# Seven block products for two of three down-projections, and the sample tile moved to the first block

## The chip, the cores and the metric

The kernel runs on one core of one Trainium2 chip. The metric is the device time of one execution in microseconds (us); three runs of the kernel before gave 2807.08, 2808.53 and 2813.18 us, so its median is 2808.53 us. Five engines work side by side, each through its own list of instructions in order: PE (TensorE, matrix products; its weight loads are listed as PEld), DVE (VectorE), ACT (ScalarE), POOL (GpSimd) and SP (SyncE, which here only issues transfers). A wait on one engine holds everything behind it in that engine's list.

## The reference

One layer of a hybrid encoder works on 2048 prompt rows and 128 sample rows of width 1024. Attention, an mLSTM and an output projection come first; the change leaves them alone. What follows them is the gated feed-forward part:

```python
def conv_ffn(h, buf, w_up, w_conv, b_conv, w_down):
    u = h @ w_up                                  # 1024 -> 5632
    ext = jnp.concatenate([buf, u], axis=1)
    y = b_conv
    for j in range(3):                            # causal depthwise convolution over tokens
        y = y + ext[:, j:j + S] * w_conv[j]
    gate, up = jnp.split(y, 2, axis=-1)
    return (gelu(gate) * up) @ w_down, ext[:, S:]   # 2816 -> 1024
x = x + rms_norm(conv_ffn(rms_norm(x, g2), ...)[0], g3)
```

The sample rows are eight sequences of 16 tokens, each with its own two columns of convolution history. All arrays are fp32.

## The kernel before, in words

Rows are cut into 17 token tiles of 128 rows: tiles 0 to 15 are the prompt, tile 16 (`SAMPLE`) the sample. To keep fp32 precision from a faster format, each operand of a product is split in two: `hi` is a cast (on ACT, L1257 in `split`), `lo` is the operand minus `hi` (on DVE, L1258), and `mm3` issues three matmuls, hi·hi, hi·lo and lo·hi (L95, L96, L97).

**Stages.** The first part of the program (norms, projections, attention, mLSTM, output projection) leaves x after the mixing in DRAM tiles `x2d`. Then come three blocks of token tiles, `FBLOCKS`: six tiles, six tiles, and four with the sample. Each block has an up stage and a down stage.

- **Up stage.** It goes over 22 slices f of 128 gate and 128 up columns. The product of a slice is already made as seven block products instead of eight: the tokens in two halves of `HALF[b]` columns, the 1024 rows of the weight in two halves, gate and up as the two column halves. The tokens' sums are made once a block (`h2_units`, tiles `B0` to `B6`). The weights' four sums a slice are made on DVE in the first block (`load_quads`, L1274, tiles `ws`) and kept in DRAM (`wsd`) for the other two. A slice then needs 7 weight splits, 84 matmuls of `HALF[b]` columns (names `ua`, `ub`, `uec`), a few additions of accumulators (L1410, L1482, L1484, L1499), two convolutions (one pass on ACT, L1429, two on DVE, L1430 and L1431), and the gated product `g` (L1505), which goes to DRAM (`gd`).
- **Down stage.** For each of two 512-column halves `dh` and each of 22 steps k it fetches g (`gr`), splits it, and multiplies it for every tile of the block with the weight block of step k: 22 x 2 x 3 = 132 matmuls of 512 columns for each tile (names `dn`, `dnm`). Weights (`wdr`, split to `wdh`, `wdl`) are loaded in chunks of four steps, one chunk ahead (`load_down`). Beside this run units through `ahead`, one step per k: the preparation of the next block's tokens, and the end of the previous block's rows (`later`: norm on DVE, addition on POOL, store). In the last block the last steps are ordered tile by tile, so that each tile's end (`finish`) runs under the next tile's matmuls.

**Buffers that couple the engines.** Loads of 512 columns, sums and pieces share 11 buffers (`quad`). Rows of g share 3 (`row`). Split g has room for two steps (`w3`, 4 buffers), split weights for two chunks (`wh`, `wl`, 2 each). A scheduler fixes each engine's order when the program is built.

## Time and profile before

| | |
|---|---|
| median of three runs | 2808.53 us |
| span of the profiled execution, first to last instruction | 2794.3 us |
| median less span (no other time is recorded for the profiled execution) | 14.2 us |
| first part, to the first matmul of an up stage | 0 to 1317.6 us |
| up, down of block 1 (six tiles) | 327.9, 194.6 us |
| up, down of block 2 (six tiles) | 317.7, 198.2 us |
| up, down of block 3 (four tiles and the sample) | 269.9, 160.7 us |
| after the last matmul's start | 7.7 us |

Blocks are numbered from 1 here; in names the number is one lower (`dn1` is the second). Busy time is what an engine spends in instructions; two that overlap on one engine are counted once. The stage table gives for each stretch its length and each engine's busy time with its count of instructions; in the waits, the engine on the left stood still for what is on the right.

### The profile page before, as it was taken

The numbers are of one execution on the slowest core, as the hardware profiler recorded it, in microseconds if no ns is written. First come the engines' busy times: TensorE is split into PE (matmuls) and PEld (weight loads), VectorE is DVE, ScalarE is ACT, GpSimd is POOL, SyncE is SP. The second block draws the span as 40 slices with busy tenths as digits, with TensorE's granted clock in tenths as the row PEclk, the third lists the DMA queues.
The fourth block names the chain that finished last, engine by engine and source line by source line (L and its number), as shares of the span: only waits on it lengthen the run. The fifth ranks groups of instructions, "written<-read, shape, count | busy, mean of one in ns | idle before, by whom it ended". The sixth has DMA issues, their size and how long they took to land.

```text
span 2794.3 us, 47075 instructions
## 1 busy us (share of the span) xinstructions
PE 2728.0 (98%) x16587; PEld 2551.0 (91%) x16587; DVE 1873.5 (67%) x3442; ACT 1408.9 (50%) x2836; POOL 449.9 (16%) x876
## 2 busy tenths in 40 slices
...
GB/s 189 157 123 126 111 173 157 171 159 212 165 159 147 159 183 165 91 194 210 192 164 173 162 171 173 220 148 157 151 153 154 259 262 158 169 180 177 182 309 195
DMA packets 313419, 486.04 MB, mean 174 GB/s; under 512 B 55427, under 2 KB 150623, under 8 KB 313055
## 3 DMA queue, kind: packets, MB, share of 16 engines
...
q8 instruction: 130, 2.13, 0.3%
q14 instruction: 107, 0.87, 0.1%
...
## 4 chain that ended last, share of the span: by engine, by line
PE 52%; DVE 4%; DMA 2%; issue 2%; ACT 1%; POOL 1%; SPq 0%; DVEq 0%; POOLq 0%; ACTq 0%
PE uec L95 6%; PE uec L96 6%; PE uec L97 5%; PE dn L97 4%; PE dn L96 3%; PE dn L95 3%; PE ua L97 3%; PE ua L95 3%; PE ua L96 3%; PE dnm L95 2%; PE dnm L97 2%; PE dnm L96 2%; PE wo L95 2%; PE wo L96 2%; PE wo L97 2%
## 5 line engine op out<-in xcount | busy, mean ns | idle before, releaser
L95 PE MATMUL uec<-B,wuh 128*128 128x384 f32 (+1 forms) x720 | 236.6, 329 | 5.6 <-DVE uu L1499 4.7
L96 PE MATMUL uec<-B,wuh 128*128 128x384 f32 (+1 forms) x720 | 235.4, 327 | 0.0
L97 PE MATMUL uec<-B,wul 128*128 128x384 f32 (+1 forms) x720 | 233.5, 327 | 0.0
L1258 DVE TENSOR_TENSOR gl<-gr,gh 128x768 fp32r<-128x768 f32 (+3 forms) x141 | 118.3, 846 | 158.6 <-ACT gh L1257 158.2
L1257 ACT CAST gh<-gr 128x768 fp32r<-128x768 f32 (+3 forms) x141 | 102.1, 736 | 211.5 <-PE dn L96 178.3
L1257 ACT CAST wuh<-wu 128x512 fp32r<-128x512 f32 x255 | 141.8, 617 | 91.2 <-PE uec L96 87.3
L95 PE MATMUL dn<-wdh,gh 128*128 128x512 f32 x466 | 182.6, 392 | 2.4 <-DVE ug L1410 2.4
L96 PE MATMUL dn<-wdl,gh 128*128 128x512 f32 x466 | 183.6, 394 | 0.0
L97 PE MATMUL dn<-wdh,gl 128*128 128x512 f32 x466 | 168.5, 396 | 0.0
L1258 DVE TENSOR_TENSOR wul<-wu,wuh 128x512 fp32r<-128x512 f32 x255 | 164.7, 685 | 2.8 <-DMA x2d<-mx 2.8
L393 DVE CUSTOM_DVE_ANT_0 tmp<-s,nb 128x640 f32<-128x640 f32 (+4 forms) x128 | 94.5, 738 | 95.8 <-PE s L383 95.2
L95 PE MATMUL vo<-wi_h,hT 128*128 128x256 f32 x544 | 156.0, 287 | 0.6 <-DVE mt L199 0.6
L97 PE MATMUL vo<-wi_h,hT 128*128 128x256 f32 x544 | 156.4, 287 | 0.0
L96 PE MATMUL vo<-wi_l,hT 128*128 128x256 f32 x544 | 155.5, 286 | 0.0
L95 PEld LDWEIGHTS uec<-B,wuh 128*128 128x128 f32 x720 | 135.3, 188 | 9.9 <-DVE uu L1499 6.7
L96 PEld LDWEIGHTS uec<-B,wuh 128*128 128x128 f32 x720 | 135.5, 188 | 0.1
L97 PEld LDWEIGHTS uec<-B,wul 128*128 128x128 f32 x720 | 135.2, 188 | 0.0
L95 PE MATMUL qk<-hT,wi_h 128*128 128x384 f32 (+1 forms) x384 | 128.5, 335 | 4.3 <-ACT qk_st L224 3.4
L406 DVE TENSOR_TENSOR ptl<-pt,pth 128x640 fp32r<-128x640 f32 (+4 forms) x128 | 93.7, 738 | 57.6 <-ACT pth L405 56.5
L394 ACT ACTIVATE tmp<-tmp,mn 128x640 f32<-128x640 f32 (+4 forms) x128 | 97.6, 763 | 63.0 <-DVE mn L393 60.5
L96 PE MATMUL qb<-hT,wi_h 128*128 128x384 f32 (+1 forms) x384 | 128.0, 333 | 0.0
L96 PE MATMUL qk<-hT,wi_h 128*128 128x384 f32 (+1 forms) x384 | 127.6, 332 | 0.0
...
## 6 DMA issues: line engine op xcount, KB each, us to landing
wu<-in_w_up SPq DMA_DIRECT2D x220, 256.0 KB, 3.9
wu<-wsd SPq DMA_DIRECT2D x176, 256.0 KB, 4.0
wdr<-in_w_down SPq DMA_DIRECT2D x132, 256.0 KB, 5.5
...
wsd<-ws SPq DMA_DIRECT2D x88, 256.0 KB, 2.8
...
```

The costliest lines, as they stand in the source:

```text
L95: nc.tensor.matmul(out, ah, bh, start=start, stop=False, skip_group_check=onto)
L96: nc.tensor.matmul(out, ah, bl, start=False, stop=False, skip_group_check=onto)
L97: nc.tensor.matmul(out, al, bh, start=False, stop=stop, skip_group_check=onto)
L393: nc.vector.tensor_tensor_reduce(o_, s_, b_, 1.0, 3e38, ALU.add, ALU.min, accum_out=mn)
L394: nc.scalar.activation(tmp[:, :n], tmp[:, :n], AF.Exp, bias=mn, scale=-1.0, accum_out=rsum[:, i % 4, hh:hh + 1])
L406: nc.vector.tensor_tensor(s.ptl[:, sl, qc], ptv, s.pth[:, sl, qc], op=ALU.subtract)
L1257: nc.scalar.copy(h, r)
L1258: nc.vector.tensor_tensor(l, r, h, op=ALU.subtract)
```

## The change

**The blocks** become four tiles with the sample (0 to 3, 16), tiles 4 to 9, tiles 10 to 15. The sample's special paths (`samp`) move to the first block with it, and `HALF` is 320, 384, 384.

**The first block's down stage** stays as it was (`plain`), without the tile-by-tile end. It also makes the sums of the down weights: in every other chunk `load_down` loads the other half's two 512-column blocks of each pair of steps, 22 loads `wt` in all, and `step_sums` makes 4 sums for each of 11 pairs on DVE (L1349) and stores them to `wtd` (L1350).

**The other two down stages** are made as seven products D1, D6, D2, D7, D5, D4, D3 of half as many tiles (3), half as many steps (11) and 512 columns. Each product has 6 units q of two steps (the last one of one step): 42 units, 77 weight blocks, 33 of them raw and 44 sums, and 7 x 11 x 3 x 3 = 693 matmuls. Weights are loaded four blocks at a time for two units (`load_block`). The tokens' seven operands come from the up stage: three are pieces of g, and for every second slice DVE makes four sums of 384 columns (tile `gs`) that go with them to DRAM (`gsd`). After each product three accumulators are copied or added into `dx` tiles; `keep` takes the squares. In the last block the tiles 13 to 15 are finished before D3 (`finish_now`), and D3's last two units are ordered tile by tile.

An argument of the program's builder, `dynamic_dma_scratch_size`, is set to 1024; the profile's list of transfers shows issues from SP and ACT alone.

```diff
-FBLOCKS = [[0, 1, 2, 3, 4, 5], [6, 7, 8, 9, 10, 11], [12, 13, 14, 15, SAMPLE]]
-HALF = [384, 384, 320]
-PAIRS = [[(((b[j], 0), (b[j + 3], 0)), j * P, P, f"{b[j]}") for j in range(3)] for b in FBLOCKS[:2]]
-PAIRS += [[(((12, 0), (15, 0)), 0, P, "12"), (((13, 0), (SAMPLE, 0)), P, P, "13"), (((14, 0), (14, 64)), 2 * P, 64, "14")]]
+FBLOCKS = [[0, 1, 2, 3, SAMPLE], [4, 5, 6, 7, 8, 9], [10, 11, 12, 13, 14, 15]]
+HALF = [320, 384, 384]
+PAIRS = [[(((0, 0), (3, 0)), 0, P, "0"), (((1, 0), (SAMPLE, 0)), P, P, "1"), (((2, 0), (2, 64)), 2 * P, 64, "2")]]
+PAIRS += [[(((b[j], 0), (b[j + 3], 0)), j * P, P, f"{b[j]}") for j in range(3)] for b in FBLOCKS[1:]]
...
     def load_down(dh, c):
-        n = 4 if c < 5 else 2
-        src = I["w_down"][dh, 2 * c:2 * c + n // 2].rearrange("a p n -> p a n")
-        h_ = wpool.tile([P, 2112], F32R, tag="wh", name=f"wdh{dh}_{c}", bufs=2)
-        l_ = wpool.tile([P, 2112], F32R, tag="wl", name=f"wdl{dh}_{c}", bufs=2)
-        for a in range(n // 2):
-            for e in range(2):
-                cc = slice(a * 1024 + e * 512, a * 1024 + e * 512 + 512)
-                raw = quad(f"wdr{dh}_{c}_{a}_{e}")
-                nc.sync.dma_start(raw, src[:, a, e * 512:e * 512 + 512])
-                split(h_[:, cc], l_[:, cc], raw)
-        return h_, l_
+
+        ks = range(4 * c, 4 * c + (4 if c < 5 else 2))
+        at = lambda k, h: ((0, 1), (3, 2))[k % 2][h]
+        raws_ = []
+        w = load_w([block_of(I["w_down"], k // 2, at(k, dh)) for k in ks], f"{dh}_{c}", raws_)
+        if c % 2 == dh:
+            for x, k in enumerate(ks):
+                if k % 2:
+                    continue
+                t = [None] * 4
+                for e in range(2):
+                    t[at(k + e, dh)] = raws_[x + e]
+                    r = t[at(k + e, 1 - dh)] = quad(f"wt{k + e}")
+                    nc.sync.dma_start(r, block_of(I["w_down"], k // 2, at(k + e, 1 - dh)))
+                for o, x_, y_, op in ((2, 2, 1, ALU.subtract), (1, 1, 0, ALU.subtract), (0, 2, 0, ALU.add),
+                                      (3, 3, 0, ALU.subtract)):
+                    sums.append((t, o, x_, y_, op, wtd[k // 2][:, KEPT_AT[o] * 512:KEPT_AT[o] * 512 + 512]))
+        return w
...
+    def step_sums(count):
+        for _ in range(min(count, len(sums))):
+            t, o, x_, y_, op, dst = sums.popleft()
+            nc.vector.tensor_tensor(t[o], t[x_], t[y_], op=op)
+            nc.sync.dma_start(dst, t[o])
+
+    D1, D6, D2, D7, D5, D4, D3 = range(7)
+    W_RAW, W_SUM = 0, 1
+    D_WEIGHT = {D1: (W_RAW, 0), D2: (W_RAW, 3), D3: (W_RAW, 2), D5: (W_SUM, 0), D7: (W_SUM, 1), D6: (W_SUM, 2),
+                D4: (W_SUM, 3)}
+    D_TOKENS = {D1: 0, D2: 1, D4: 2, D5: 3, D6: 4, D7: 5, D3: 6}
...
+    def load_block(b, q):
+        p, c = divmod(q, 3)
+        kind, at = D_WEIGHT[p]
+        src = (I["w_down"], wtd)[kind]
+        return load_w([block_of(src, i, at) for i in range(4 * c, min(4 * c + 4, NF // 2))], f"{b}_{q}")
...
+            half = lambda t, i: t[:, i * n:(i + 1) * n]
+            to = gsd[b][f // 4][:, :, f // 2 % 2 * 384:f // 2 % 2 * 384 + 384]
+            if f % 2 == 0:
+                nc.sync.dma_start(to[:, 0, :], half(gt, 0))
+                even = gt
+                continue
+            nc.sync.dma_start(to[:, 1:3, :], gt[:, :2 * n].rearrange("p (a n) -> p a n", a=2))
+            gs = p4.tile([P, 1536], F32, tag="gs", name=f"gs{nm}", bufs=2)
+            s1, s2, s3, s4 = [half(gs, i) for i in range(4)]
+            for o, x, y, op in ((s3, half(even, 0), half(even, 1), ALU.subtract),
+                                (s1, half(even, 1), half(gt, 1), ALU.add), (s2, s1, half(even, 0), ALU.subtract),
+                                (s4, half(gt, 0), s2, ALU.subtract)):
+                nc.vector.tensor_tensor(o, x, y, op=op)
+            nc.sync.dma_start(to[:, 3:7, :], gs.rearrange("p (a n) -> p a n", a=4))
...
+            for q in range(42):
+                p, u = divmod(q, 6)
+                acc = banks[(0, 1, 0, 1, 0, 1, 0)[p]]
+                onto = p in (D2, D4, D3)
+                if u % 2 == 0:
+                    wh, wl = pend
+                    if q < 40:
+                        pend = load_block(b, q // 2 + 1)
+                    elif not last:
+                        quads = [load_quads(b + 1, 0, i) for i in range(2)]
+                        pend = [load_up(b + 1, 0, 0, quads[0])]
+                if q not in parts:
+                    split_unit(q)
+                if q >= 2:
+                    fetch_unit(q + 2)
+                def multiply(u, j, k):
+                    gh, gl = parts[p * 6 + u]
+                    at = u % 2 * 1024 + k * 512
+                    tt = slice(k * 384 + j * P, k * 384 + j * P + P)
+                    mm3(acc[j], gh[:, tt], gl[:, tt], wh[:, at:at + 512], wl[:, at:at + 512],
+                        start=not onto and u == k == 0, stop=u == 5, onto=onto)
...
+                if last and q == 41:
+                    for j in range(3):
+                        for k in range(3):
+                            multiply(4 + k // 2, j, k % 2)
+                        o = x2[:, j]
+                        nc.vector.tensor_tensor(o, o, acc[j], op=ALU.add)
+                        ssq = p3.tile([P, 1], F32, tag=f"dssq{j}", name=f"dssq{tiles[j]}_1", bufs=2)
+                        nc.scalar.activation(junk, o, AF.Square, accum_out=ssq)
+                        finish(b, j, rests[j], o, o, ssq, res[j])
+                        if j == 0:
+                            rests.append(load_rest(b, 2))
+                    continue
+                for k in range(2 if u < 5 else 1):
+                    for j in range(3):
+                        multiply(u, j, k)
+                parts.pop(q)
+                if u < 5:
+                    continue
+                for j in range(3):
+                    if p == D1:
+                        nc.scalar.copy(x2[:, j], acc[j])
+                    elif p == D6:
+                        nc.vector.tensor_tensor(x2[:, j], x2[:, j], acc[j], op=ALU.add)
+                    elif p == D2:
+                        o = quad(f"c11_{b}_{j}")
+                        nc.scalar.copy(o, acc[j])
+                        keep(j, 0, o)
+                    elif p == D7:
+                        nc.vector.tensor_tensor(x3[:, j], x2[:, j], acc[j], op=ALU.add)
+                    elif p == D5:
+                        nc.vector.tensor_tensor(x3[:, j], x3[:, j], acc[j], op=ALU.add)
+                        keep(j + 3, 1, x3[:, j])
+                    elif p == D4:
+                        o = quad(f"c21_{b}_{j}")
+                        nc.vector.tensor_tensor(o, x2[:, j], acc[j], op=ALU.add)
+                        keep(j + 3, 0, o)
+                        if last:
+                            finish_now(j + 3, o, x3[:, j])
+                    else:
+                        nc.vector.tensor_tensor(x2[:, j], x2[:, j], acc[j], op=ALU.add)
+                        keep(j, 1, x2[:, j])
...
+                    step_sums(3)
```

**Order of instructions, three places.** Names: `gl` and `gh` are the split g of a step or unit, `wdl` a split weight block, `wt` and `wdr` raw weight blocks, `B`, `t` and `b` the next block's token operands and their pieces, `f` a row of the previous block being finished, numbers behind the name the block and the step or unit.

DVE, down stage of the first block, before, two steps of the first weight half:

```order
L1258 TENSOR_TENSOR gl0_0_13_20153<-gr0_0_13_20070,gh0_0_13_20152 128x768
L1258 TENSOR_TENSOR wdl0_4_20100<-wdr0_4_0_0_20101,wdh0_4_20099 128x512
L1258 TENSOR_TENSOR wdl0_4_20100<-wdr0_4_0_1_20105,wdh0_4_20099 128x512
L1258 TENSOR_TENSOR wdl0_4_20100<-wdr0_4_1_0_20109,wdh0_4_20099 128x512
L1258 TENSOR_TENSOR wdl0_4_20100<-wdr0_4_1_1_20113,wdh0_4_20099 128x512
L1118 TENSOR_TENSOR t27_20183<-h2T_pt7_1_1_20176,t17_20148 128x512
L1119 TENSOR_TENSOR t37_20184<-h2T_pt7_1_1_20176,b127_20146 128x512
L1100 TENSOR_TENSOR B6_1_19747<-b227_20181,B6_1_19747 128x4x128
L1258 TENSOR_TENSOR gl0_0_14_20194<-gr0_0_14_20121,gh0_0_14_20193 128x768
```

The same two steps with the change:

```order
L1260 TENSOR_TENSOR gl0_0_13_20354<-gr0_0_13_20263,gh0_0_13_20353 128x640
L1102 TENSOR_TENSOR B3_1_19937<-t15_20349,B3_1_19937 128x4x128
L1349 TENSOR_TENSOR wt16_20307<-wt16_20307,wdr0_4_0_20291 128x512
L1260 TENSOR_TENSOR wdl0_4_20290<-wdr0_4_0_20291,wdh0_4_20289 128x512
L1349 TENSOR_TENSOR wt19_20313<-wt19_20313,wt18_20311 128x512
L1260 TENSOR_TENSOR wdl0_4_20290<-wdr0_4_1_20295,wdh0_4_20289 128x512
L1260 TENSOR_TENSOR wdl0_4_20290<-wdr0_4_2_20299,wdh0_4_20289 128x512
L1260 TENSOR_TENSOR wdl0_4_20290<-wdr0_4_3_20303,wdh0_4_20289 128x512
L1349 TENSOR_TENSOR wdr0_4_0_20291<-wt17_20309,wdr0_4_0_20291 128x512
L1260 TENSOR_TENSOR gl0_0_14_20398<-gr0_0_14_20319,gh0_0_14_20397 128x640
```

Between the two splits of g stood seven instructions, now eight; three of them are weight sums, and pieces of the next block's tokens have moved behind.

DVE, down stage of the second block, while the next block's tokens are prepared; first before, between two steps:

```order
L1258 TENSOR_TENSOR gl1_0_9_24879<-gr1_0_9_24789,gh1_0_9_24878 128x768
L1126 TENSOR_TENSOR t412_24820<-h2T_pt12_0_1_24813,t212_24775 128x512
L1100 TENSOR_TENSOR B4_2_24593<-b2112_24818,B4_2_24593 128x4x128
L1100 TENSOR_TENSOR B5_2_24594<-t412_24820,B5_2_24594 128x4x128
L1079 SCALAR_TENSOR_TENSOR x2r13_24871<-x2r13_24871,n2_13_rs_24907,g2_15183 128x1024
L1258 TENSOR_TENSOR wdl0_3_24830<-wdr0_3_0_0_24831,wdh0_3_24829 128x512
L1079 SCALAR_TENSOR_TENSOR x2r16_24873<-x2r16_24873,n2_16_rs_24914,g2_15183 128x1024
L1258 TENSOR_TENSOR gl1_0_10_24917<-gr1_0_10_24851,gh1_0_10_24916 128x768
```

With the change, between two units:

```order
L1260 TENSOR_TENSOR gl1_15_25388<-gq1_15_25294,gh1_15_25387 128x768
L1260 TENSOR_TENSOR wdl1_8_25329<-wdr1_8_0_25330,wdh1_8_25328 128x512
L1260 TENSOR_TENSOR wdl1_8_25329<-wdr1_8_1_25334,wdh1_8_25328 128x512
L1413 SCALAR_TENSOR_TENSOR f00_25348<-f00_25348,drs0_21372,norm_row3_16222 128x512
L1102 TENSOR_TENSOR B1_2_24842<-t211_25359,B1_2_24842 128x4x128
L1260 TENSOR_TENSOR wdl1_8_25329<-wdr1_8_2_25338,wdh1_8_25328 128x512
L1102 TENSOR_TENSOR B2_2_24843<-t311_25360,B2_2_24843 128x4x128
L1128 TENSOR_TENSOR t411_25404<-h2T_pt11_0_1_25397,t211_25359 128x512
L1102 TENSOR_TENSOR B4_2_24845<-b2111_25402,B4_2_24845 128x4x128
L1413 SCALAR_TENSOR_TENSOR f10_25393<-f10_25393,drs0_21372,norm_row3_16222 128x512
L1260 TENSOR_TENSOR gl1_16_25450<-gq1_16_25346,gh1_16_25449 128x768
```

One weight split stood between the two splits of g, now three, beside the same kind of pieces.

POOL, the end of the program, the last two tiles before:

```order
L78 TENSOR_SCALAR n3_15_ms_30874<-dssq15_1_30872,dssq15_0_30276 128x1
L84 TENSOR_TENSOR n3_15_rs_30876<-n3_15_ms_30874,nhalf_74 128x1
L1357 TENSOR_TENSOR f015_30866<-f015_30866,xa15_30867 128x512
L78 TENSOR_SCALAR n3_16_ms_30911<-dssq16_1_30909,dssq16_0_30280 128x1
L84 TENSOR_TENSOR n3_16_rs_30913<-n3_16_ms_30911,nhalf_74 128x1
```

The last three tiles (10, 11, 12) with the change:

```order
L78 TENSOR_SCALAR n3_10_ms_31199<-dssq10_1_31197,dssq10_0_30399 128x1
L84 TENSOR_TENSOR n3_10_rs_31201<-n3_10_ms_31199,nhalf_74 128x1
L1403 TENSOR_TENSOR f010_31171<-f010_31171,xa10_31172 128x512
L78 TENSOR_SCALAR n3_11_ms_31227<-dssq11_1_31225,dssq11_0_30405 128x1
L84 TENSOR_TENSOR n3_11_rs_31229<-n3_11_ms_31227,nhalf_74 128x1
L78 TENSOR_SCALAR n3_12_ms_31249<-dssq12_1_31247,dssq12_0_30411 128x1
L84 TENSOR_TENSOR n3_12_rs_31251<-n3_12_ms_31249,nhalf_74 128x1
L1403 TENSOR_TENSOR f011_31177<-f011_31177,xa11_31178 128x512
L1403 TENSOR_TENSOR f012_31209<-f012_31209,xa12_31210 128x512
```

The addition of tile 10 now stands ahead of the norms (`ms`, `rs`) of tiles 11 and 12, and the last two additions behind both.

189 lines of the change are left out of this document (124 added, 65 removed).

## The prediction

> **What bounds the kernel now.** I read the page's busy times first, then the stage table, then the matmuls' pace, then DVE's groups and waits in the first block.
>
> ```profile
> span 2794.3 us, 47075 instructions
> PE 2728.0 (98%) x16587; PEld 2551.0 (91%) x16587; DVE 1873.5 (67%) x3442; ACT 1408.9 (50%) x2836; POOL 449.9 (16%) x876
> ```
>
> PE is busy for 98% of the span, DVE for 67%. A mean over stages hides which engine has room where, so the stage table follows (length; busy time of PE, PEld, DVE, ACT, POOL; clock, DMA share, GB/s). Its rows are block 1 up and down, block 2 up and down, block 3 up and down, the end, and a stretch of block 3's down.
>
> ```profile
> 1317.60:1645.50 327.90, 321.23 (x1824) 316.68 (x1823) 300.96 (x454) 166.62 (x266) 70.42 (x87) 1.00 0.54 177
> 1645.50:1840.10 194.60, 193.41 (x868) 157.91 (x867) 112.14 (x154) 95.54 (x160) 8.85 (x22) 1.00 0.56 184
> 1840.10:2157.80 317.70, 317.70 (x1825) 317.67 (x1823) 245.73 (x366) 162.75 (x270) 42.94 (x96) 1.00 0.48 154
> 2157.80:2356.00 198.20, 195.14 (x867) 157.17 (x866) 121.39 (x165) 91.09 (x156) 31.81 (x34) 1.00 0.67 226
> 2356.00:2625.90 269.90, 269.12 (x1837) 268.86 (x1836) 233.09 (x476) 155.62 (x274) 70.68 (x182) 1.00 0.55 177
> 2625.90:2786.60 160.70, 155.58 (x674) 125.48 (x672) 94.15 (x130) 62.48 (x107) 30.86 (x31) 1.00 0.72 251
> 2786.60:2794.30 7.70, 0.18 (x1) 0.00 (x0) 2.98 (x4) 0.69 (x2) 2.08 (x3) 0.68 0.41 153
> 2655.00:2724.00 69.00, 69.00 (x301) 56.43 (x300) 39.89 (x53) 28.75 (x49) 14.44 (x14) 1.00 0.84 308
> ```
>
> Two things are to be seen. PE sets the length of every stage, at full clock (1.00). But in block 1's up stage DVE is busy 300.96 of 327.90 us (0.918): that stage also makes the weight sums, and it is 10.2 us longer than the same products in block 2 (317.70). There PE has almost no lead over DVE.
>
> PE's pace, from two matmuls of block 2's down stage with eight starts between them:
>
> ```profile
> 2201.50 0.39 PE L96 MATMUL dn<-wdl,gh 128*128 128x512 f32 x1
> 2203.35 0.39 PE L96 MATMUL dnm<-wdl,gh 128*128 128x512 f32 x1
> ```
>
> A 512-column matmul costs 1.85 / 8 = 0.231 us. An up stage of 1848 matmuls takes 317.7 us with 384 columns and 269.9 us with 320.
>
> **Part 1: the products.** The down stages go from 792 + 792 + 660 = 2244 matmuls to 660 + 693 + 693 = 2046. The order of instructions shows these counts, so that the change might not do what it says is out. 198 x 0.231 = 45.8 us of PE work goes: 132 x 0.231 = 30.5 us from block 1 (one tile less), 99 x 0.231 = 22.9 from block 2, and block 3 gains 33 x 0.231 = 7.6.
>
> **Part 2: the short up stage moves to block 1.** On PE alone the three up stages still add up to the same. But block 3's becomes 317.7 instead of 269.9 (47.8 us more), and block 1's can fall from 327.9 only as far as DVE lets it. DVE's groups in block 1's up stage:
>
> ```profile
> L1258 DVE TENSOR_TENSOR wul<-ws,wuh 128x512 fp32r<-128x512 f32 x58 | 38.6, 686 | 0.0
> L1274 DVE TENSOR_TENSOR ws<-wu,wu 128x512 f32<-128x512 f32 x42 | 28.9, 687 | 7.1 <-DMA wu<-in_w_up 7.1
> L1431 DVE SCALAR_TENSOR_TENSOR y<-uu,wcv,y 128x768 f32<-128x768 f32 x21 | 21.3, 1013 | 0.1
> L1505 DVE TENSOR_TENSOR g<-y,y 128x768 f32<-128x768 f32 x20 | 19.1, 954 | 0.0
> L1482 DVE TENSOR_TENSOR x<-x,ub 128x384 f32<-128x384 f32 x22 | 12.1, 549 | 0.0
> L1144 DVE TENSOR_TENSOR B<-B 128x1536 fp32r<-128x1536 f32 x4 | 6.8, 1748 | 0.0
> ```
>
> and the same kinds in block 3's, with the sample and 320 columns:
>
> ```profile
> L1431 DVE SCALAR_TENSOR_TENSOR y<-uu,wcv,y 128x656 f32<-128x656 f32 x21 | 18.9, 898 | 0.3
> L1505 DVE TENSOR_TENSOR g<-y,y 128x512 f32<-128x512 f32 x20 | 13.7, 687 | 2.4 <-ACT y L1433 2.2
> L1482 DVE TENSOR_TENSOR x<-x,ub 128x320 f32<-128x320 f32 x22 | 10.6, 482 | 4.1 <-PE ub L97 2.0 <-ACT x L1480 1.8 <-issue 0.3
> L1410 DVE TENSOR_TENSOR uu<-x,uec 128x128 f32<-128x128 f32 x44 | 12.4, 283 | 3.9 <-PE uec L97 3.8
> L1410 DVE TENSOR_TENSOR uu<-x,uec 128x64 f32<-128x64 f32 x22 | 4.7, 215 | 0.0
> ```
>
> Durations overlap where nothing is waited for: a sum that takes 0.69 is followed 0.60 us later.
>
> ```profile
> 1500.60 0.69 DVE L1274 TENSOR_TENSOR ws<-ws,wu 128x512 f32<-128x512 f32 x1
> 1501.20 0.69 DVE L1274 TENSOR_TENSOR ws<-wu,wu 128x512 f32<-128x512 f32 x1
> ```
>
> So I count each instruction's duration less 0.08. A slice's four convolution passes save 4 x 0.116 = 0.46 us and three additions 3 x 0.067 = 0.20. The two additions into halves become three each: 2 x (0.20 + 0.20 + 0.14 - 0.47) = 0.14 more. The product in two pieces gives 0.61 + 0.20 for 0.87, 0.06 less. Net 0.58 less; over 22 slices, with 1.1 for the four late `B` splits (1280 columns for 1536), 300.96 becomes 287. From block 3's side, 233.09 plus 88 sums of 0.60 (52.8) plus 5.8 for the `B` splits give 291.7. I take the higher, 291.7 us of DVE work. It is more than PE's 269.9: **DVE becomes the bound of block 1's up stage.** What stands on top is DVE's own standing still:
>
> ```profile
> DVE ug L1410 <- PE uec L97: 7.9, 8, 1.9
> DVE ws L1274 <- DMA wu<-in_w_up: 7.1, 11, 2.1
> DVE y L1430 <- ACT y L1429: 7.0, 6, 1.2
> DVE uu L1499 <- PE uec L97: 2.1, 4, 1.1
> DVE uu L1410 <- PE uec L97: 1.3, 2, 0.6
> ```
>
> The 11.3 us of waits for PE should mostly go, since PE will be early. The 14.1 for loads and for ACT have other causes; I keep them in a stage some 6% shorter, 14.1 x 0.94 = 13.3: 291.7 + 13.3 = 305.0, bounds 293 (all waits go) and 317.8 (DVE's busy share stays 0.918).
>
> [...]
>
> **Part 3: sums of g in blocks 2 and 3.** Per block 44 subtractions of 384 columns at 0.549 - 0.08 = 0.47: 20.7 us, so DVE has 245.7 + 20.7 = 266 us in 317.7. Block 2 lost nothing at 245.7, block 1 some 10 us at 301. I put 0.8 us on each stage (bounds 0 and 4): 318.5.
>
> **Part 4: block 1's down stage.** 194.6 - 30.5 = 164.1. Its 44 weight sums (44 x 0.60 = 26.4 us) raise DVE to 112.1 + 26.4 - 5.9 (44 g splits of 640 columns for 768) - 1.2 (two copies less) = 131.4 us of 164.1: room on the mean. Locally there is none: in the order shown above, eight instructions stand between two splits of g, 8 x 0.60 + 0.74 = 5.5 us where PE needs 15 x 0.231 = 3.5 a step. Split g reaches two steps ahead, so most such bursts are caught. I put 4.5 us (bounds 0 and 11): 168.6.
>
> **Part 5: the product stages.** A unit is 18 matmuls, 4.2 us, as a step was. Weight splits go from 44 to 77 a block: 33 x 0.60 = 20 us more on DVE. Block 2's DVE comes to 121.4 + 20 - 4.6 (35 splits of g at 0.87 and 7 at 0.47 for 44 at 0.87) + about 6 (one more tile to prepare, half a pair's work at the rate of the others, an estimate) = 143 us in 175. While a pair of tiles is prepared it is full: in the order shown, nine instructions plus a split are 9 x 0.61 + 0.87 = 6.4 us for a unit of 4.2. Loads of weights now come every two units (8.3 us) where they came every four steps (16.7). The transfer list of block 2's down stage (x count, size, us to landing) and SP's issues there:
>
> ```profile
> wdr<-in_w_down SPq DMA_DIRECT2D x36, 256.0 KB, 5.6
> ```
>
> ```profile
> 2211.26 1.85 SPq L1312 DMA_DIRECT2D wdr<-in_w_down  x4
> ```
>
> Four loads take 1.85 us to issue and 5.6 to land, 7.5 together, under 8.3 even with no lead; and SP may run ahead as far as the 11 buffers allow. Queued behind a late load on SP are the fetches of g and the stores of finished rows. Bytes: block 2 moved 226 x 198.2 = 44.8 MB; 33 blocks of 0.262 MB more and some 2 less of g give 51 MB in 179 us, 285 GB/s; block 3, by the same count, to about 305. The stretch at 308 GB/s had PE busy 69.00 of 69.00, so volume is no bound. Block 2: 198.2 - 22.9 + 4 = 179.3 (bounds 173 and 190). Block 3, with finished rows but no tiles to prepare: 160.7 + 7.6 + 1 = 169.3 (bounds 166 and 180).
>
> **Part 6: the end.** Three tiles now end within 6.2 us of matmuls, first and second together, where each had 4.2. After the last matmul before:
>
> ```profile
> 2786.87 0.60 ACT L1334 ACTIVATE junk<-dn 128x512 f32<-128x512 f32 x1 [4.06 <-issue]
> ```
>
> ```profile
> 2787.66 0.27 POOL L78 TENSOR_SCALAR n_ms<-dssq,dssq 128x1 f32<-128x1 f32 x1 [1.23 <-ACT junk L1334]
> 2788.00 0.55 POOL L84 TENSOR_TENSOR n_rs<-n_ms,nhalf 128x1 f32<-128x1 f32 x1
> 2789.41 1.26 POOL L1357 TENSOR_TENSOR f<-f,xa 128x512 f32<-128x512 f32 x1 [0.86 <-DVE f L1355]
> ```
>
> POOL has three norms of about 0.9 and three additions of 1.3, 6.6 us in line, with tile 10's addition ahead of the other norms; DVE's last additions wait for it. I put the end at 10.7 instead of 7.7 (bounds 9 and 13).
>
> **The sum.** 1317.6 + 305.0 + 168.6 + 318.5 + 179.3 + 318.5 + 169.3 + 10.7 = 2787.5 us of span, 6.8 less than 2794.3. The first part is kept: its order is the same up to the last few tiles. The 14.2 us between span and median are kept too: 2808.5 - 6.8 = **2801.7 us**, own range 2793 to 2811. Less than 0.2% (5.6 us) a measurement of this kernel can't tell from no change.
>
> **The rivals.** *DVE takes the gain* (slower): in block 1's up stage DVE keeps its busy share of 0.918, since its in-order waits for ACT and for loads stay and those for PE come back through the accumulators. That is 317.8 instead of 305.0: 2814.5. For it: the waits above. Against: with PE early they should shrink. It decides from a busy share of 0.935 downward (291.7 / 0.935 = 312, 6.8 over my 305). *The queues absorb everything*: block 1's up at 293, no new stalls in the down stages: 2801.7 - 12 - 9.5 - 1.6 = about 2779. For it: block 3's first stretch at 308 GB/s without a stall; against: the crowded orders above. *The products starve* (slower): loads or their splits come late by 0.5 us at each of 2 x 21 chunks: 21 us, 2823. For it: the halved lead; against: 7.5 us is under 8.3. [...]
>
> **How the numbers follow.** Forecast 0.48 (faster 0.25, same 0.23), DVE takes the gain 0.20 (slower 0.12, same 0.08), queues absorb 0.17 (faster), products starve 0.12 (slower 0.10, same 0.02), latency exposed 0.03 (slower). Together: faster 0.42, same 0.33, slower 0.25. The range 2782 to 2822 takes in the first two and about half of the next two.
>
> **What would show it.** Right: block 1's up stage near 305 us with DVE busy over 0.95 and PE waiting for DVE; its down stage near 169; product stages near 179 and 169 with PE busy over 0.96; up stages of 318 us. Wrong: block 1's up at 318 or more, a product stage beyond 190 with PE waiting for `wdl` or `gl`, or an end beyond 13 us.

## The result and the profile after

The changed kernel takes **2842.5 us** (2836.8 to 2846.3) against 2809.7 us for the kernel before, a ratio of 1.0119 [1.0107, 1.0131]: slower by 33 us, where 7 us faster was forecast, and outside the range. The head of its page:

```profile
span 2840.6 us, 47269 instructions
PE 2711.6 (95%) x16389; PEld 2530.6 (89%) x16389; DVE 1979.6 (70%) x3643; ACT 1439.9 (51%) x2908; POOL 458.2 (16%) x878
```

The 198 matmuls are gone (16587 to 16389), but PE's busy time fell by only 16.4 us and the span grew by 46.3. By stage (the columns are those of the prediction's table: stretch, length, busy time of PE, PEld, DVE, ACT, POOL, then clock, DMA share and GB/s; the last row is a stretch inside block 2's down stage):

```profile
0.00:1325.30 1325.30, 1277.39 (x8704) 1207.72 (x8705) 759.21 (x1698) 671.75 (x1604) 190.00 (x419) 0.99 0.51 157
1325.30:1628.30 303.00, 277.45 (x1825) 270.23 (x1823) 284.78 (x555) 156.52 (x264) 92.22 (x170) 0.99 0.56 186
1628.30:1813.50 185.20, 169.58 (x735) 134.66 (x734) 131.58 (x206) 91.01 (x159) 13.81 (x27) 0.97 0.83 269
1813.50:2134.30 320.80, 320.08 (x1837) 319.71 (x1836) 267.67 (x410) 162.97 (x271) 44.32 (x95) 1.00 0.54 172
2134.30:2319.00 184.70, 174.08 (x758) 140.91 (x757) 141.72 (x198) 109.92 (x195) 34.14 (x37) 0.97 0.82 275
2319.00:2639.60 320.60, 319.88 (x1836) 319.52 (x1835) 266.41 (x409) 162.90 (x268) 42.27 (x91) 1.00 0.53 171
2639.60:2827.40 187.80, 173.13 (x707) 137.80 (x705) 119.79 (x164) 83.35 (x145) 34.69 (x33) 0.95 0.76 262
2827.40:2840.60 13.20, 0.00 (x0) 0.00 (x0) 8.49 (x10) 1.44 (x4) 6.75 (x7) 0.69 0.32 119
2151.50:2164.50 13.00, 8.58 (x29) 6.58 (x28) 10.39 (x15) 6.72 (x12) 2.28 (x4) 0.74 0.80 262
```

| part | forecast, us | measured, us | difference |
|---|---|---|---|
| first part | 1317.6 | 1325.3 | +7.7 |
| three up stages | 305.0 + 318.5 + 318.5 | 303.0 + 320.8 + 320.6 | +2.4 |
| block 1 down | 168.6 | 185.2 | +16.6 |
| block 2 down | 179.3 | 184.7 | +5.4 |
| block 3 down | 169.3 | 187.8 | +18.5 |
| end | 10.7 | 13.2 | +2.5 |

The up stages came out as forecast. The down stages are 40.5 us over it: they lost 45.8 us of matmul work and together are 4 us *longer* than before (557.7 against 553.5). What ended PE's waits there, for block 1, 2 and 3 (total us, times, longest):

```profile
PE dnm L95 <- ACT gh L1259: 10.5, 5, 3.7
...
PE h2T_pt L1089 <- DVE x2r L1081: 4.7, 2, 4.0
PE dn L95 <- ACT gh L1259: 4.4, 1, 4.4
...
PE dn L96 <- DVE wdl L1260: 6.4, 2, 4.0
PE dn L95 <- ACT gh L1259: 4.9, 1, 4.9
```

These are few stalls, most of them of 2 to 5 us, not many small ones. And most cost more than their length. The timeline of PE around the one at 2153 us:

```profile
2153.03 0.40 PE L97 MATMUL dnm<-wdh,gl 128*128 128x512 f32 x1
2157.84 0.79 PE L95 MATMUL dn<-wdh,gh 128*128 128x512 f32 x1 [4.42 <-ACT gh L1259]
2158.44 0.63 PE L96 MATMUL dn<-wdl,gh 128*128 128x512 f32 x1
```

After 4.42 us without work the matmuls take 0.63 to 0.79 us, not 0.40, and start 0.43 us apart, not 0.23: the granted clock is 0.74 on the mean of these 13 us (last row of the table above), 6.8 us at half speed. The clock records put the first 1.2 of these inside the stall, so some 5.6 us of matmuls ran at half speed, and 2.8 us were lost beside the 4.42. In block 1's down stage the clock is 0.97, so 2 x 0.03 x 185.2 = 11 us ran at half clock and 5.6 us of work were lost; in block 3's, at 0.95, 2 x 0.05 x 187.8 = 19 us and 9.4. Before, every down stage read 1.00.

### The profile page after: what moved, and what is told of

Same layout as the page of the kernel before. It is cut to its first block, busy times and chain, and to the rows that moved or that the text cites. A ratio compares the mean times of both kernels' runs of the same rounds, so it can differ in the third digit from the quotient of the medians.

```text
span 2840.6 us, 47269 instructions
## 1 busy us (share of the span) xinstructions
PE 2711.6 (95%) x16389; PEld 2530.6 (89%) x16389; DVE 1979.6 (70%) x3643; ACT 1439.9 (51%) x2908; POOL 458.2 (16%) x878
## 5 line engine op out<-in xcount | busy, mean ns | idle before, releaser
L95 PE MATMUL uec<-B,wuh 128*128 128x384 f32 (+1 forms) x720 | 237.8, 331 | 20.5 <-DVE uu L1457 10.5
L96 PE MATMUL dn<-wdl,gh 128*128 128x512 f32 x440 | 177.6, 404 | 6.4 <-DVE wdl L1260 6.4
L1260 DVE TENSOR_TENSOR wdl<-wdr,wdh 128x512 fp32r<-128x512 f32 x198 | 129.0, 695 | 19.8 <-ACT wdh L1259 19.5
L1259 ACT CAST gh<-gq 128x768 fp32r<-128x768 f32 (+1 forms) x92 | 66.3, 729 | 140.1 <-PE dnm L96 61.5
L95 PE MATMUL qk<-hT,wi_h 128*128 128x384 f32 (+1 forms) x384 | 128.9, 336 | 8.0 <-ACT qk_st L226 7.4
L1259 ACT CAST wdh<-wdr 128x512 fp32r<-128x512 f32 x198 | 112.1, 617 | 41.8 <-DMA wdr<-in_w_down 15.0
L1260 DVE TENSOR_TENSOR gl<-gq,gh 128x768 fp32r<-128x768 f32 (+1 forms) x92 | 79.5, 875 | 70.6 <-ACT gh L1259 70.5
```

The lines of the kernel that those rows point to most:

```text
L95: nc.tensor.matmul(out, ah, bh, start=start, stop=False, skip_group_check=onto)
L96: nc.tensor.matmul(out, ah, bl, start=False, stop=False, skip_group_check=onto)
L1259: nc.scalar.copy(h, r)
L1260: nc.vector.tensor_tensor(l, r, h, op=ALU.subtract)
```

## Experiments

Each ratio is against the kernel before, run on the same chip beside it. Its median was 2809.4, 2807.1, 2806.3, 2804.4 and 2803.1 us in the five groups of runs e1 to e18, so ratios are compared, not times. The columns d1 to d3 are the down stages of blocks 1 to 3, each from one profile. How far such a length can be trusted is seen where the stage's own code was left alone: block 1's took 181.9 to 185.2 us (changed kernel, e1, e7, e13), block 2's 178.5 to 184.7 us and block 3's 186.7 to 187.8 us (changed kernel, e4, e6, e9); in e5, where only the place in DRAM that part of the weights come from differs there, they took 184.9 and 184.3 us. A difference inside these spans shows nothing.

| run | us | ratio [95%] | d1 | d2 | d3 |
|---|---|---|---|---|---|
| changed kernel | 2842.5 | 1.0119 [1.0107, 1.0131] | 185.2 | 184.7 | 187.8 |
| e1 unit 4 early | 2840.8 | 1.0112 [1.0097, 1.0127] | 181.9 | 179.6 | 186.3 |
| e2 order of blocks only | 2832.4 | 1.0083 [1.0068, 1.0098] | 168.7 | 194.5 | 192.1 |
| e3 products in the middle only | 2808.1 | 0.9994 [0.9980, 1.0008] | 204.0 | 183.1 | 165.7 |
| e4 sums on POOL | 2857.9 | 1.0178 [1.0154, 1.0201] | 179.1 | 178.5 | 187.6 |
| e5 no weight sums | 2830.8 | 1.0074 [1.0053, 1.0096] | 169.6 | 184.9 | 184.3 |
| e6 no additions | 2840.8 | 1.0111 [1.0089, 1.0134] | 182.1 | 179.5 | 186.7 |
| e7 stores on POOL's queue | 2844.7 | 1.0123 [1.0091, 1.0155] | 183.0 | 183.8 | 186.1 |
| e8 e3 + unit 4 early | 2804.3 | 0.9982 [0.9969, 0.9995] | 205.6 | 181.4 | 164.3 |
| e9 stores of sums off SP | 2846.6 | 1.0143 [1.0124, 1.0161] | 190.4 | 184.4 | 186.9 |
| e10 fetches off SP | 2849.7 | 1.0157 [1.0140, 1.0174] | 181.1 | 190.7 | 189.9 |
| e11 both off SP | 2858.7 | 1.0191 [1.0174, 1.0208] | 182.9 | 199.2 | 189.5 |
| e12 e8 + both off SP | 2808.8 | 1.0004 [0.9994, 1.0013] | 206.6 | 183.4 | 165.4 |
| e13 half of g fetched | 2839.0 | 1.0122 [1.0102, 1.0141] | 182.7 | 184.2 | 182.1 |
| e14 four row buffers, fetch further ahead | 2823.8 | 1.0068 [1.0051, 1.0084] | 175.5 | 179.1 | 185.5 |
| **e15 e8 + the same** | **2784.8** | **0.9934 [0.9914, 0.9953]** | 197.5 | 176.0 | 161.6 |
| e16 before + the same | 2798.4 | 0.9976 [0.9964, 0.9988] | 195.0 | 197.3 | 161.5 |
| e17 thirteen 512-column buffers | 2830.5 | 1.0100 [1.0085, 1.0115] | 179.3 | 181.4 | 185.4 |
| e18 four row buffers only | 2827.7 | 1.0092 [1.0075, 1.0109] | 177.3 | 176.4 | 184.2 |

**e2: the order of the blocks alone.** Edit, on the kernel before:

```diff
-FBLOCKS = [[0, 1, 2, 3, 4, 5], [6, 7, 8, 9, 10, 11], [12, 13, 14, 15, SAMPLE]]
+FBLOCKS = [[0, 1, 2, 3, SAMPLE], [4, 5, 6, 7, 8, 9], [10, 11, 12, 13, 14, 15]]
```

(with the tables of halves and pairs that go with it; all down stages plain).

> The kernel before with the blocks of the change alone (five tiles with the sample first, then six and six), all down stages plain, no weight sums for them. Theory (DVE bounds the first up stage): the first up stage takes 300 to 306 us instead of 327.9, the last 318 instead of 269.9, the down stages as many matmuls as before: some 23 us slower than before, 2832. Rival (PE is the bound everywhere, and the changed kernel lost its time in the product stages alone): first up stage 275 or less, time within 6 us of before.

```profile
1329.70:1632.70 303.00, 279.65 (x1825) 271.86 (x1823) 283.94 (x556) 157.49 (x265) 94.61 (x171) 0.98 0.57 185
1632.70:1801.40 168.70, 163.54 (x736) 131.88 (x735) 105.37 (x160) 89.85 (x159) 14.21 (x25) 1.00 0.60 195
2119.10:2313.60 194.50, 193.32 (x867) 157.68 (x866) 122.77 (x164) 94.74 (x157) 29.78 (x32) 1.00 0.68 225
2631.30:2823.40 192.10, 188.90 (x818) 152.71 (x817) 104.37 (x133) 70.51 (x115) 33.83 (x35) 1.00 0.67 233
```

The reorder costs 23 us by itself: the up stages add up to 303.0 + 317.7 + 317.7 = 938.4 us for 915.5, since the block that makes the weight sums is now the short one and waits for DVE. So the products and the sums, which by the forecast were to take some 31 us off (2801.7 against e2's 2832.4), add another 10 on top. Against e2, block 1's down stage (same products, plus the weight sums) is 16.5 us longer, of which 10.4 is more idle time of PE and 6.0 more busy time at a lower clock; blocks 2 and 3 lose 22.9 us of matmul work each, and only 9.8 and 4.3 us of time.

**e1: the fetch of unit 4.** In blocks 2 and 3, g's unit 4 is fetched before the last slice's store and not behind it, into 512-column buffers instead of a row buffer (it is what PE waited for in the stall at 2153 us above):

```diff
-                for q in range(2, 4):
+                for q in range(2, 5):
...
-                if q >= 2:
+                if q >= 3:
```

> One edit to the changed kernel: the fetch of unit 4 of each product stage is issued with those of units 2 and 3, ahead of the last slice's stores of g, into the 512-column buffers. Theory (transfers are held in SP's list behind stores that wait for DVE, and each stall of PE is followed by a stretch at half clock): the stalls of 4.4 and 4.9 us at the entry of the two product stages go, and with them 6.8 us at half clock behind each (3.4 us lost each): 8.1 + 8.3 = 16 us less, 2826 us, at least 8 us less. Rival (the volume of transfers at 270 us GB/s and more is what makes g late): the fetch lands late wherever it stands, less than 3 us gained, 2840.

Ratio 1.0112, hardly less than 1.0119. Block 2's stall went; its stage took 179.6 us, which is inside the spread given above. In block 3 a stall of 6.3 us appeared three units on, on ACT's copy of a later unit of g. Removing one late transfer shows the next.

**e3 and e8: products in the second block alone**, in the old order 6, 6, 5; e8 with the early fetch too.

```diff
-FBLOCKS = [[0, 1, 2, 3, SAMPLE], [4, 5, 6, 7, 8, 9], [10, 11, 12, 13, 14, 15]]
+FBLOCKS = [[0, 1, 2, 3, 4, 5], [6, 7, 8, 9, 10, 11], [12, 13, 14, 15, SAMPLE]]
...
-        plain = samp = b == 0
+        plain, samp = b != 1, last
```

> Blocks as in the kernel before (six, six, five with the sample last); the first block's down stage makes the weight sums, the second's alone is made as seven products, the third stays plain with its old end. Theory: 22.9 us of matmuls less; stalls and half clock at the entry of the product stage about 8 us, bursts there and in the first down stage 5 to 12: 0 to 10 us faster than before, 2799 to 2809. Rival (a product stage costs more than it saves, whatever the order of the blocks): slower than before by 5 us or more, 2814 and up.

> The kernel with the order of blocks as before (6, 6, 5), weight sums in the first block and products in the second alone, which took 2808.1 us against 2809.4 us, now with unit 4's g fetched early in the second block. Theory: the stalls of 4.29 us and 4.37 us at product and plain stages' unit 4 are this fetch, and one is followed by 6.8 us at half clock; with the first gone the second block's down stage falls from 183 us to about 174 us and the time to 2799 us (2794 to 2804). Rival: the stall is replaced by one on ACT's copy of g a few units on, as in the changed kernel with the same edit; then 2805 us or more.

0.9994 and 0.9982, between the two expectations for e8. Without the reorder the idea breaks even: the second block gains, the first pays for the sums (204.0 and 205.6 us for 194.6 before).

**e5 and e6: what of the weight sums costs.** e5 leaves all of them out, e6 only the additions:

```diff
 e5
-        if c % 2 == dh:
+        if False:
...
-        src = (I["w_down"], wtd)[kind]
+        src = I["w_down"]
 e6
-            nc.vector.tensor_tensor(t[o], t[x_], t[y_], op=op)
```

> The changed kernel without the weight sums of block 1's down stage: no extra loads, no additions on VectorE, no stores of the sums. The products of blocks 2 and 3 then multiply by blocks of the weights themselves, so this run leaves the sums out of the computation; its instructions in blocks 2 and 3 are the same in number and size. Theory: the sums are what makes block 1's down stage 185.2 us where the same stage without them took 168.6 us in the run with only the order of blocks changed. Then the stage goes to 167 to 171 us and the time from 2842.5 us to 2826 us (2820 to 2832). Rival: the stage's length comes from where half-clock stretches fall, which any change of order shifts; then the stage stays above 178 us and the time above 2836 us.

> The changed kernel with the loads and the stores of the weight sums kept and only VectorE's additions left out (the buffer that is stored holds none of the sums, so this run leaves them out of the computation). Theory: what costs in block 1's down stage is the 44 additions on VectorE, which stand ahead of the copies that PE and ACT wait for. Then the stage is 167 to 172 us and the time 2824 to 2831 us, as in the run without any part of the sums. Rival: it is the transfers (264 KB more per chunk on the queues, and stores that wait in SP's order); then the stage stays at 180 us or more and the time at 2836 us or more.

Block 1's down stage of e5, then of e6:

```profile
1636.20:1805.80 169.60, 163.84 (x735) 131.88 (x734) 105.61 (x160) 89.88 (x159) 12.78 (x25) 1.00 0.62 194
```

```profile
1634.00:1816.10 182.10, 169.04 (x734) 136.32 (x733) 106.08 (x160) 90.48 (x159) 15.11 (x25) 0.96 0.80 272
```

Leaving out everything takes 15.6 us off the stage (and 0.0045 off the ratio); leaving out the additions takes 3, which is no more than the spread. So my theory for e6 fell: DVE's 44 additions are not what costs, the transfers of the sums are. The transfers of that stage, changed kernel and e5:

```profile
DMA packets 25110, 49.80 MB, mean 269 GB/s; under 512 B 2783, under 2 KB 3423, under 8 KB 25097
```

```profile
DMA packets 15690, 32.96 MB, mean 194 GB/s; under 512 B 1735, under 2 KB 1863, under 8 KB 15679
```

Half as many bytes again, in a stage with one tile less. But which of three things makes them late: their order on SP, their volume, or the buffers that they pass through? What SP waited for in that stage of the changed kernel seems to speak for the first:

```profile
SPq L1501 <- DVE gl L1260: 20.5, 15, 3.8
SPq L1350 <- DVE wt L1349: 15.0, 14, 3.3
...
SPq L1350 <- DVE wdr L1349: 9.5, 11, 2.0
SPq L1313 <- DMA wtd<-wdr: 9.0, 8, 2.6
```

L1350 is the store of a sum, L1313 a weight load, L1501 a fetch of g. But such waits say little by themselves. In e5, where the stage is 15.6 us shorter, SP stood three times as long at the fetches of g:

```profile
SPq L1501 <- DVE gl L1260: 67.9, 29, 4.5
```

SP stands there because it is ahead of the engines. Whether a wait of SP costs time is seen only where PE stalls behind it, or when it is taken away.

**e7, e9 to e12: the order on SP.** These move issues from SP's queue to POOL's: e7 the stores of finished rows (on top of e1), e9 the stores of the sums, e10 the fetches of g, e11 both, e12 both in e8.

```diff
 e9
-            nc.sync.dma_start(dst, t[o])
+            nc.gpsimd.dma_start(dst, t[o])
 e10
-                nc.sync.dma_start(g[q], src)
+                nc.gpsimd.dma_start(g[q], src)
```

> The changed kernel with unit 4's g fetched early (as in the run before this one) and with the stores of finished rows issued from POOL's queue and not from SP's. Theory: in the product stages SP stands at a store of finished rows that waits for an addition, and the weight and g loads behind it come late; with the stores on the queue of the engine that makes the additions, SP is free, block 3's down stage goes from 187.8 us to about 176 us and block 2's from 184.7 us to about 178 us, and the time from 2842.5 us to 2826 us (2818 to 2833). Rival: POOL is then late with the additions themselves and PE stalls on what they free, or the stalls go to other places as they did when only the fetch was made earlier; then 2836 us or more.

> The changed kernel with the 44 stores of the weight sums issued from POOL's queue and not from SP's; nothing else. Theory: in block 1's down stage SP stands 24.5 us at these stores (15.0 and 9.5 us, waiting for VectorE's additions), and the weight and g loads behind them come late, which is where the stage's 185.2 us against 168.6 us come from. Then the stage falls to about 173 us and the time from 2842.5 us to 2831 us (2826 to 2836). Rival: it is the transfers themselves or the eleven 512-column buffers that they hold; then the stage stays above 180 us and the time above 2837 us.

> The changed kernel with the fetches of g in all down stages issued from POOL's queue, so that on SP no weight load stands behind a fetch that waits for its buffer; nothing else. Theory: in block 3's product stage SP stands 42.8 us at 23 such fetches (the longest 3.8 us), and the weights come late behind them; block 2's down stage falls from 184.7 us to about 177 us, block 3's from 187.8 us to about 179 us, and the time to 2825 us (2817 to 2833). Rival: g itself is late because its three buffers come free late, whatever the queue; then stalls on ACT's copies of g stay, and the time is 2837 us or more.

> The changed kernel with both the stores of the weight sums and the fetches of g on POOL's queue. Theory: the two parts add, 11 us and 17 us, and the time is about 2814 us (2806 to 2824); what is left above the kernel before is the first up stage, which VectorE bounds. Rival: POOL's own queue is then the one that stands, with additions of finished rows behind it; 2830 us or more.

> The kernel with the order of blocks as before (6, 6, 5), weight sums in the first block, products in the second alone and unit 4's g fetched early, which took 2804.3 us against 2807.1 us, now with the stores of the sums and the fetches of g on POOL's queue. Theory: the first block's down stage (203 us there) loses some 10 us of stalls and half-clock stretches, the second's and third's some 3 us each, and the time is 2792 us (2786 to 2799). Rival: POOL's queue stalls in its turn, as above; 2802 us or more.

Five misses: each came out in its rival's numbers. None is faster than its parent, and e10 and e11 are clearly slower. In e9 SP no longer stands at the stores, yet it stands as long at what comes next:

```profile
SPq L1501 <- DVE gl L1260: 42.7, 19, 6.4
SPq L1313 <- DMA wtd<-wdr: 18.2, 7, 4.4
```

The fetch now waits 42.7 us (20.5 before) until `gl` has been made out of the row buffer that it wants, and the weight load 18.2 us (9.0 before) until a stored sum has left its buffer. As said, waits of SP are weak evidence; the ratio, no better than the changed kernel's, is the stronger. It speaks against the order on SP, but does not settle it, for two reasons. The moved transfers also changed their kind of queue; in e9's block 1 they are listed apart from SP's `hardware_dynamic` queue (packets, MB, share of the DMA engines' time):

```profile
q0 software_dynamic: 3440, 11.27, 17.1%
```

And POOL's queue was no free one: in e10's block 2 unit 4's fetch stood behind an addition of a finished row,

```profile
2152.54 1.86 POOL L1414 TENSOR_TENSOR f<-f,x 128x512 f32<-128x512 f32 x1 [1.34 <-ACT wdh L1259]
2154.34 1.09 POOL L1525 DMA_DIRECT2D gq<-gsd  x2
```

and PE waited for it 8.8 us instead of 4.4. Nor was ACT's queue, the other one that the kernel issues from, tried.

**e13 and e14: volume or buffers.** Fetches of g go through three 1024-column row buffers; a spare 4 KB per partition allows a fourth. e13 fetches half the bytes through the same three and makes both halves of each operand from them; e14 fetches all through four, three units ahead and not two, with unit 4 early as in e1.

```diff
 e13
-                g[q] = row(f"gq{b}_{q}")[:, :w]
-                nc.sync.dma_start(g[q], src)
+                g[q] = row(f"gq{b}_{q}")[:, :w // 2]
+                nc.sync.dma_start(g[q], src[:, :w // 2])
 e14
-        return ffn.p3.tile([P, D], F32, tag="yq", name=name, bufs=3)
+        return ffn.p3.tile([P, D], F32, tag="yq", name=name, bufs=4)
...
-                    fetch_unit(q + 2)
+                    fetch_unit(q + 3)
...
-                        fetch(dh + (k + 2) // NF, (k + 2) % NF)
+                        fetch(dh + (k + 3) // NF, (k + 3) % NF)
```

> The changed kernel with only the first half of each of g's columns fetched in the product stages (the other half of each unit is taken from the same half, so this run leaves half of g out of the products; PE, ACT and VectorE do the same work on the same sizes). Theory of volume: block 2's down stage moves 50.7 MB in 184.7 us with the DMA engines 81% busy, where the plain stage of the same block moves 43.9 MB in 194 us at 68%; with some 8 MB less per stage the transfers land in time, block 2's down stage falls to about 176 us and block 3's from 187.8 us to about 178 us, and the time to 2824 us (2817 to 2831). Rival: the fetch is late because its buffer comes free late and the store of the last slice stands ahead of it; then both stages stay within 4 us and the time is 2835 us or more.

> The changed kernel with four 1024-column row buffers and not three, and g fetched three units ahead and not two, in all down stages (unit 4 of the product stages early). Theory of buffers: stalls on the copies of g go, block 1's down stage falls from 185.2 us to about 176 us, block 2's and block 3's by about 8 us each, and the time to 2820 us (2810 to 2829). Rival (volume): the same bytes are moved by engines that are 82% busy, and the stalls move to the weights and the finished rows; 2834 us or more.

The product stages of e13 (blocks 2 and 3), then the down stages of e14 (blocks 1, 2, 3):

```profile
2142.90:2327.10 184.20, 172.58 (x757) 138.32 (x756) 141.19 (x198) 111.18 (x195) 33.29 (x37) 0.99 0.72 239
2647.70:2829.80 182.10, 169.40 (x706) 135.80 (x704) 125.68 (x163) 83.78 (x145) 34.76 (x33) 0.96 0.69 233
```

```profile
1631.20:1806.70 175.50, 165.09 (x735) 133.49 (x734) 131.56 (x205) 90.67 (x159) 19.11 (x26) 0.99 0.85 284
2127.60:2306.70 179.10, 172.01 (x756) 138.45 (x756) 140.02 (x199) 110.36 (x196) 35.04 (x37) 0.99 0.83 284
2627.30:2812.80 185.50, 171.08 (x705) 135.82 (x705) 120.62 (x164) 83.90 (x146) 33.90 (x33) 0.96 0.78 266
```

Half the fetched bytes (DMA share 0.72 for 0.82, in as many packets) change block 2's stage by 0.5 us and the ratio not at all; block 3's falls by 5.7, short of the 10 us that volume was to give, but more than any other edit took off this stage, so there a share of volume is not excluded. All the bytes through one more buffer, fetched earlier, take 14 us off by ratio (0.0051), with intervals well apart; block 1's stage falls by 9.7 us, at a *higher* rate (284 GB/s). So in blocks 1 and 2 the bytes are not the limit, and buffer and distance together are worth 14 of the 33 us. e14's block 2 stands at 179.1 us, the forecast's 179.3, but so did e1's with three buffers (179.6) and e6's with nothing changed there (179.5), so this stage alone does not show what the buffer does.

**e17 and e18: which buffer.** e17 gives the same 4 KB to the 512-column buffers (`bufs=11` to 13), e18 is e14 with the fetches where they were.

> The changed kernel with thirteen 512-column buffers and not eleven (raw weights, the blocks of the sums and finished rows go through them), and three row buffers as it has; nothing else. In the run with four row buffers block 3's down stage stayed at 187 us, its stalls now on the copies of the weights (ACT wdh, VectorE wdl). Theory: these weights come late because finished rows hold the 512-column buffers; with two more block 3's down stage falls from 187.8 us to about 182 us and block 1's, where the sums use them, from 185.2 us to about 181 us, block 2's little, and the time to 2832 us (2825 to 2837). Rival: the stalls on g, which these buffers don't touch, take what the weights gain; 2838 us or more.

> The changed kernel with four row buffers, but g still fetched two units ahead, and unit 4 where it was. Theory: it is the buffer that comes free late, since the fetch for unit k+2 must wait for the copy of unit k-1 out of the same buffer; with four the fetch goes as soon as it is issued, and most of the 18.7 us of the run with four rows comes with it: 2829 us (2822 to 2835). Rival: it is the distance of the fetch, and the fourth buffer alone does nothing: 2838 us or more.

e18's fourth buffer alone shortens blocks 1 and 2 by 7.9 and 8.3 us; its ratio, 1.0092 against 1.0119, is 7 of the 14 us that e14 gains by ratio, with intervals that just touch. e17's two 512-column buffers gain 5 us by ratio (1.0100), with 5.9 us in block 1, where the sums go through them. The intervals of e17 and e18 overlap almost wholly, so the runs show that 4 KB more of buffers help, and not which buffer was the narrow one. The other 7 us of e14 come with the distance and the early unit. Block 3's stage moves by 2.4 and 3.6 us, about as much as in e5. And e18 keeps a stall of 4.1 us at block 2's unit 4, which e1 removes: there it is the fetch's place on SP, or the other buffers that e1 gives it, and not the number of row buffers.

**e4: the weight sums on POOL.** Both kinds of sums, those of the up stage too, as additions on POOL:

```diff
-            nc.vector.tensor_tensor(t[o], t[x_], t[y_], op=op)
+            nc.gpsimd.tensor_tensor(t[o], t[x_], t[y_], op=op)
```

> The changed kernel with the sums of the up weights (88) and of the down weights (44) on POOL instead of DVE. Theory (DVE's work is what bounds the first up stage and crowds the first down stage): DVE loses 53 us in the up stage and 27 in the down stage; the up stage falls from 303 to 270 to 280, the down stage from 185 to 172 to 180: 30 to 45 us less than the changed kernel, 2798 to 2812. Rival (POOL's sums, 1.3 us each, slow DVE or are late themselves): first up stage at 295 or more, 2835 or more.

The slowest but one of all. Block 1's up stage became 330 us. DVE's subtractions there, in e2 and then in e4, and POOL's sums in e4:

```profile
L1258 DVE TENSOR_TENSOR wul<-ws,wuh 128x512 fp32r<-128x512 f32 x60 | 39.8, 679 | 0.0
```

```profile
L1260 DVE TENSOR_TENSOR wul<-ws,wuh 128x512 fp32r<-128x512 f32 x60 | 58.1, 990 | 0.0
L1276 POOL TENSOR_TENSOR ws<-wu,wu 128x512 f32<-128x512 f32 x42 | 65.2, 1553 | 39.1 <-DMA wu<-in_w_up 25.7 <-DVE wul L1260 6.5 <-DVE wu L1260 3.4
```

The two engines slow each other: 0.68 to 0.99 us on DVE, and on POOL 1.55 us for a sum, where the four additions of finished rows of the same size that have nothing beside them on DVE in the changed kernel's trace take 1.28 to 1.29. The runs show the slowing, not what causes it.

**e15 and e16: the version that beats both.** e15 is e8 with four row buffers and the longer distance; e16 the kernel before with the same, to tell the buffer from the products.

> The kernel with the order 6, 6, 5, sums in the first block, products in the second alone and unit 4 fetched early, which took 2804.3 us, now with four row buffers and g fetched three units ahead. Theory of buffers: 2793 us (2787 to 2799), by one stall and half-clock stretch less in each of its three down stages. Rival (volume): 2801 us or more.

> The kernel before with four row buffers and g fetched three units ahead. Its down stages move fewer bytes (186 GB/s, DMA engines 57% busy in the first), and PE stalls little there; both theories expect little: 2803 us (2798 to 2809).

e15's down stages of blocks 1 and 2:

```profile
1651.30:1848.80 197.50, 194.05 (x867) 157.80 (x866) 135.16 (x193) 94.80 (x158) 9.81 (x23) 1.00 0.77 260
2169.70:2345.70 176.00, 170.94 (x758) 137.81 (x757) 138.11 (x200) 107.11 (x194) 32.92 (x39) 0.99 0.86 295
```

0.9934 [0.9914, 0.9953]: 19.6 us faster than before by the medians, 13.6 us faster than e16 on the same chip, and faster than its forecast. e16's blocks 1 and 2, for comparison:

```profile
1646.10:1841.10 195.00, 193.38 (x867) 157.77 (x866) 110.37 (x152) 95.55 (x158) 7.89 (x22) 1.00 0.55 181
2158.90:2356.20 197.30, 194.93 (x867) 157.04 (x866) 119.52 (x165) 90.59 (x155) 28.60 (x34) 1.00 0.68 227
```

With the buffer the weight sums cost 2.5 us in the first block (197.5 for 195.0, one profile each), and the products save 21.3 in the second (176.0 for 197.3), nearly all of the 22.9 us of matmul work that they remove, at 295 GB/s and nearly full clock. In e16 itself the buffer does nothing for the plain down stages (553.8 us together, 553.5 before); where its 0.0024 comes from stays open.

## Why the prediction was wrong

**Part 1 (products) was right** in its count: 198 matmuls, 45.8 us of work, went. That PE would be free to use the room was for parts 4 and 5 to show, and there it failed: PE's stalls and the half clock behind them took it all.

**Part 2 (the short up stage) was right**, and its number had some luck. 305.0 was forecast and 303.0 measured; but DVE's 291.7 us of work came out at 284.8, and its 13.3 us of standing still at 18.2, two misses that nearly cancel. PE waited for DVE there, as said, and the rivals "DVE takes the gain" (317.8) and "latency exposed" (no overlap of DVE's durations) are out: at 1497.5 us two sums of 0.68 us still start 0.60 apart. DVE's busy share is 0.94, just under the 0.95 that I asked for. e2 shows this step alone: +23 us.

**Part 3 (sums of g)** came out 2.2 us over, inside its bounds: 320.7 for 318.5 in both blocks.

**Part 4 (block 1's down stage) failed**: 4.5 us were allowed for its 44 sums and 21.1 came, 16.6 more and outside the bounds of 0 to 11. I sized the term by DVE's additions and called DVE's bursts the risk. DVE's work was forecast well (131.4 us, 131.6 measured), but e6 shows that the additions are worth 3 us at most, and e5 against e6 that their loads and stores are worth the other 12. The step counted the instructions and had no term for the 16.8 MB that come and go with them, through eleven 512-column buffers and SP, although part 5 counts bytes for its own stages. More buffers take 6 to 10 us back (e17, e18, e14).

**Part 5 (product stages) failed** in block 3: its allowance of 1 us came out at 19.5, and the stage beyond its bound of 180. Block 2's 184.7 is 5.4 us over, but inside its bounds, and unchanged code gave 178.5 to 184.7 there. Its bandwidth argument held for block 2 (e13: half of g's bytes change nothing; e15's stage ran at 295 GB/s with the clock at 0.99). The rate of 305 GB/s that it gave block 3 was too high: the 49.2 MB that this stage moved make 291 in 169.3 us. What failed is "7.5 under 8.3 even with no lead; and SP may run ahead as far as the 11 buffers allow": I compared latency with period for the *weights* and left out that g passes through *three row buffers*, each free only when `gl` has been made from it, and that unit 4's fetch stands on SP behind the last slice's store (e1). Most of the long stalls are at ACT's copy of g. In block 3, SP stood at such fetches for 42.8 us, 23 times:

```profile
SPq L1525 <- DVE gl L1260: 42.8, 23, 3.8
```

That shows which buffer the fetch waits for, not that the wait costs: SP stood longer in e5's fast stage. What shows the cost is e14's 14 us by ratio. In block 3 buffers gave at most 3.6 us, so most of its 18.5 us has no shown cause. One piece is the stall of 4.0 us near 2806 us, which no run with products in this block removed (4.0 to 6.3 us in all of them). The timeline of DVE there, and ACT's copy of the weights:

```profile
2801.10 0.75 DVE L1634 SCALAR_TENSOR_TENSOR c<-c,n_rs,norm_row 128x512 f32<-128x512 f32 x1
2801.77 1.78 DVE L1634 SCALAR_TENSOR_TENSOR dx<-dx,n_rs,norm_row 128x512 f32<-128x512 f32 x1
...
2806.04 1.75 DVE L1634 SCALAR_TENSOR_TENSOR dx<-dx,n_rs,norm_row 128x512 f32<-128x512 f32 x1
2807.72 3.43 DVE L1260 TENSOR_TENSOR wdl<-wdr,wdh 128x512 fp32r<-128x512 f32 x2
...
2806.83 0.62 ACT L1259 CAST wdh<-wdr 128x512 fp32r<-128x512 f32 x1 [1.09 <-DMA wdr<-in_w_down]
```

Six scalings of finished rows stand ahead of the weights' split, and once POOL adds beside them each takes 1.75 us instead of 0.75, the slowing that e4 shows; the split itself takes 1.7 us a block instead of 0.68. But a load of weights was late as well: ACT's copy waited for it until 2806.8, when PE had already stood for over a microsecond. How much each adds is not shown, since no run took either away. Why the first units of block 3 stall by 2 to 5 us, on g or (in e14) on weights, even with four buffers, stays open too.

**No part had the clock in it.** Every term was an idle time, and PE was taken to run at 0.231 us a matmul after it. Over the clock records of all twenty traces, from 60 us after the start on, I counted the stalls of PE with a half-clock stretch that began between the stall's start and 3.5 us after its end: 16 of 189 stalls of 1 to 1.5 us, 37 of 175 of 1.5 to 2 us, 44 of 73 of 2 to 2.5 us, 44 of 50 of 3 to 3.5 us, 48 of 48 of 3.5 to 4.5 us. Most such stretches last 3.4 us, about half of those after stalls of 3.5 to 4.5 us 6.8. So the stall of 4.4 us above cost 4.4 + 2.8, and the same idle time in pieces under a microsecond seldom costs anything on top (22 of 441 stalls of 0.5 to 1 us). More than half of the stalls of 2 to 2.5 us were enough.

**Part 6** came to 13.2, past its upper bound of 13 by a little.

**The base** was off as well. The 14.2 us between the profiled span and the median were kept as time outside the span; in the changed kernel that time is 2842.35 - 2840.6 = 1.75 us. The profiled execution of before was a short one: its first part is the shortest of the twenty traces, in which the same instructions took 1317.6 to 1334.7 us, with 6.8 to 30.7 us of them at half clock. By stages the forecast missed by 53.1 us, by medians by 40.8.

**The rival nearest the truth** was "products starve", with a chance of 0.12, and it was mis-sized: it had 0.5 us at each of 42 chunks, for the weights, where there were few stalls of 2 to 5 us, most of them for g, most with a tail at half clock.
